# First FFN projection of a two-layer block: 20 pairs of column tiles by seven half-sized products, gated output in DRAM

## The chip, the cores and the metric

The kernel runs on one core of a Trainium2 chip, as one launch. The metric is device time in microseconds (us) of a whole execution. The core has a matrix engine (TensorE, "PE" in the profile, with its weight loads as "PEld"), three engines for element-wise work (VectorE "DVE", ScalarE "ACT", GpSimd "POOL") and SyncE ("SP"), whose queue ("SPq") issues all the DMAs of this kernel. TensorE writes its results to PSUM, from where DVE and ACT read them.

## The reference

Two blocks run one after the other on x of 1024 tokens by 1024 features, in float32. The first block is a gated mixer with convolutions, the second one has attention, a spatial gating unit and a feed-forward network (FFN). The change is in the FFN at the very end:

```python
def conv_gated_mlp(h, w_up, conv_w, conv_b, w_down):
    z = h @ w_up                                  # [1024, 1024] @ [1024, 5632]
    zp = jnp.pad(z, ((0, 0), (CONV_WIDTH - 1, 0), (0, 0)))
    zc = conv_b
    for tap in range(CONV_WIDTH):                 # 3 taps along the tokens
        zc = zc + conv_w[tap] * zp[:, tap:tap + S]
    gate, val = jnp.split(zc, 2, axis=-1)
    return (jax.nn.silu(gate) * val) @ w_down     # [1024, 2816] @ [2816, 1024]
...
x = x + conv_gated_mlp(rmsnorm(x, ffn_norm[l]), w_up[l], conv_w[l], conv_b[l], w_down[l])
```

## The kernel before

Features lie on the 128 partitions, tokens along the free dimension. Every float32 operand of TensorE is held as a pair hi + lo of a reduced type: hi is a rounded copy made by ACT, lo is the difference made by DVE (`hilo`, L110). A product of two such operands is three matmuls, hi hi, hi lo and lo hi (`mm3`), each 128x128 by 128x512.

The work is a list of slots (`Slot`), which `run` walks in order, and each engine executes its instructions in the order in which they are written; nothing is moved by a planner. A slot has weights to fetch (`ws`), matmuls (`mm`), an epilogue (`epi`) and a few hooks (`pre`, `mid`), and it can take some tasks from a queue of background work after its matmuls (`bg`). Weights run ahead of use: `dma_ahead` keeps two raw tiles in flight on SP, and `split_ahead`, called at the start of each slot, splits the weights of the slot after the next one into hi and lo, once their two buffers are free. Work that has been written earlier into DVE's or ACT's order stands ahead of such a split.

The FFN begins in the last part of the output phase of the second block. The first three column tiles of `w_up` (gate 0, value 0, gate 1) are done in halves of 512 tokens, slots uh0.0, uh1.0, uh2.0, uh0.1, uh1.1 and uh2.1, with the last transpose of H (the normalised input, as hi and lo, `self.H`) after uh0.0. Then tile up1.1 and 40 further tiles follow, gate and value in turn, 22 of each in all. Each is 2 halves x 8 k-blocks x 3 = 48 matmuls into one pair of PSUM banks (`pair`, 128x1024). Its epilogue `up_epi` is an ACT pass that applies one tap with the bias (z), two DVE passes for the other taps (L108), and then Silu on ACT for a gate or, for a value tile, the multiplication with its gate into `G` on DVE (L1435; the last one on POOL). `G` holds all 22 gated tiles of 128x1024 in on-chip memory (SBUF).

The down projection (`down`) takes two halves of 512 tokens with 22 steps each. A step splits one half row of `G` (gh, gl) and one row of `w_dn` (wh, wl), and adds 24 matmuls to eight PSUM banks, three pairs and two single banks (`bank`). At the end of a half the residual is added and the result stored.

Of the kernel before, what the change touches and what calls it, by code (L numbers as in the profile page):

```python
# [20 lines left out]
H = 512  # L21
# [30 lines left out]
class Slot:  # L52
    def __init__(self, ws=(), mm=None, epi=None, pre=None, bg=0, split=None, mid=None, dst=None,
                 name=""):
        self.dst = dst
        self.name = name
        self.mid = mid
        self.post = False
        self.ws = list(ws)
        self.mm = mm  # L60
        self.epi = epi
        self.pre = pre
        self.bg = bg
        self.split = split


class Kernel:
# [7 lines left out]
    def pool(self, name, bufs=1, **kw):  # L75
        return self.tc.tile_pool(name=name, bufs=bufs, **kw)

# [74 lines left out]
    def mm3(self, out, a, b, first, last):  # L152
        (ah, al), (bh, bl) = a, b
        self.mul(out, ah, bh, start=first, stop=False)
        self.mul(out, ah, bl, start=False, stop=False)
        self.mul(out, al, bh, start=False, stop=last)
# [17 lines left out]
    def bank(self):  # L174
        return self.pp.tile([P, H], F, tag="pm", name="pm", bufs=2)

    def run(self):
# [8 lines left out]
        def dma_ahead():  # L186
            while st["dma"] < len(reqs) and st["dma"] < st["split"] + N_RAW:
# [3 lines left out]
                self.nc.sync.dma_start(t[:, :n], reqs[r][1])  # L191
                raws[r] = t
                st["dma"] += 1

        def split_ahead(ahead=N_HL):
            while st["split"] < min(len(reqs), st["used"] + ahead):
# [20 lines left out]

        self.release = release
        self.dma_ahead, self.split_ahead, self.hl = dma_ahead, split_ahead, hl
        for i, s in enumerate(slots):  # L220
            if s.pre:
                s.pre()
            split_ahead()
# [17 lines left out]

    def setup(self):
        nc, I, ctx = self.nc, self.I, self.ctx
        self.pp = ctx.enter_context(self.pool("psum", 3, space=bass.MemoryType.PSUM))
        self.dram = ctx.enter_context(self.pool("dram", 1, space=bass.MemoryType.DRAM))
        self.cp = ctx.enter_context(self.pool("const"))
        self.ws = ctx.enter_context(self.pool("ws"))
# [22 lines left out]
    def body(self):  # L270
        self.setup()
        self.block1()
        self.block2()
        self.ffn()
        self.run()
        self.ca.close()
        self.cb.close()

# [471 lines left out]
    def out_phase(self, blk):  # L750
# [665 lines left out]

    def up_epi(self, f, side, ps):
        nc = self.nc
        if self.G is None:
            self.G = []  # L1420
            self.reopen("cf", "cgc")
            ga, gb = self.big("B1", F), self.big("A0", F)
            gc = self.base.tile([P, 6, 1024], F, name="gc")
            self.G = [g[:, i] for g, n in ((gc, 6), (ga, 8), (gb, 8)) for i in range(n)]
        ct = f + NF * side
        z = self.c1.tile([P, 1024], F, tag="z%d" % side, name="z", bufs=2)
        w = lambda k: self.par("conv_w", ct * 3 + k)
        self.act(z, ps, AF.Identity, bias=self.par("conv_b", ct), scale=w(2))
        self.stt(z[:, 1:1024], ps[:, 0:1023], w(1), z[:, 1:1024], ALU.mult, ALU.add)
        self.stt(z[:, 2:1024], ps[:, 0:1022], w(0), z[:, 2:1024], ALU.mult, ALU.add)  # L1430
        if side == 0:
            self.act(z, z, AF.Silu)
            self.zg = z
        else:
            (nc.vector if f < NF - 1 else nc.gpsimd).tensor_tensor(self.G[f], self.zg, z, ALU.mult)  # L1435

    def ffn(self):
        nc, I = self.nc, self.I
        self.G = None
        for n in range(3, 2 * NF):  # L1440
            f, side = n // 2, n % 2
            s = {}

            def mm(w, s=s):
                s["ps"] = self.pair()
                self.mm_std(s["ps"], w, *self.H)

            self.slots.append(Slot([I["w_up"][f + NF * side]], mm, mid=self.last_half if n == 3 else None,
                                   epi=lambda f=f, side=side, s=s: self.up_epi(f, side, s["ps"]), name="up%d.%d" % (f, side)))

        st = {}

        def down(hf, fs):
# [4 lines left out]
            def split(f):  # L1458
                gh = self.c1.tile([P, H], R, tag="gh", name="gh", bufs=2)
                gl = self.c1.tile([P, H], R, tag="gl", name="gl", bufs=2)  # L1460
                self.hilo(gh, gl, self.G[f][:, hs])
                g[f] = (gh, gl)
# [8 lines left out]
            def mm(*ws):  # L1471
                if fs[0] == 0:
                    prs = [self.pair() for _ in range(3)]
                    o = [pr[:, i * H:(i + 1) * H] for pr in prs for i in range(2)]
                    st["o"] = o[:4] + [self.bank(), self.bank()] + o[4:]
# [9 lines left out]

            def pre():
                if fs[0] == NF - 6:
# [4 lines left out]
            def epi():  # L1492
                if not end:
                    return
                for b in range(8):
                    if b == 5 and hf == 0:
# [7 lines left out]
                                   split=[lambda f=f: split(f) for f in fs], name="dn%d.%d" % (hf, fs[0])))  # L1504

        def open_d():
            self.reopen("cd")

# [88 lines left out]
```

## Time and profile before

| | us |
|---|---|
| time of three runs: median (lowest to highest) | 2809.13 (2806.71 to 2809.36) |
| profiled execution: span from its first to its last instruction | 2806.2 |
| TensorE busy in that span | 2765.9 (99%) |
| DVE busy | 1390.0 (50%) |
| ACT busy | 813.3 (29%) |
| half slots of the first FFN tiles and up1.1, 2084.0 to 2122.2 | 38.2 |
| the 40 column tiles from up2.0 on, 2122.2 to 2557.4 | 435.2 |
| down projection, from 2557.4 to its last matmul at 2801.4 | 244.0 |

The profile gives of the profiled execution its span; its own time, with what lies around the span, is not recorded apart from it. The median of the three runs is 2.9 us above the span.

In timeline rows the columns are start in us, duration in us, engine, line, operation, output tile <- input tiles, shapes and count; in brackets stands how long the engine had been idle and what released it. Consecutive instructions of a kind are merged into one row. Rows of groups give count, busy time and the mean of one in ns, then idle time ahead of them. Rows of stretches give for PE, PEld, DVE, ACT and POOL the busy us and the count, then the granted TensorE clock as a share of full speed, the share of DMA engines busy and GB/s. "pp" is a pair of PSUM banks, "pm" a single one. A and B are the large SBUF buffers, here the hi and lo part of H.

### The profile page before, as it was taken

Reading aid. Unit: us, or ns where it says so; the run is one execution under the profiler, and the core shown is the slowest. Engines: PE = TensorE matmul, PEld = TensorE weight load, DVE = VectorE, ACT = ScalarE, POOL = GpSimd, SP = SyncE. Lnnn points to the kernel's source line nnn. Section 1 sums busy time; section 2 is a strip of 40 time slices with the busy share of each in tenths; the row PEclk is TensorE's granted clock in tenths of the full one; section 3 lists DMA queues with packets and bytes.
Section 4 is the critical chain, followed back from the end, with each engine's and each line's share of the span. In section 5 each row is a group of like instructions: output and inputs, shape, how many; then the busy total and the mean of one; then the engine's idle time right before and its main releaser. Section 6 shows DMA issues by size and latency. Waiting matters only on the chain.

```text
span 2806.2 us, 29345 instructions
## 1 busy us (share of the span) xinstructions
PE 2765.9 (99%) x12420; PEld 2277.9 (81%) x12420; DVE 1390.0 (50%) x1450; ACT 813.3 (29%) x1038; POOL 139.9 (5%) x132
## 2 busy tenths in 40 slices
PE   5999999999999999999999999999999999999999
PEld 3888888888888888888887788888888888887887
DVE  6898888841244422532474255537634343433343
ACT  6322222221122211421343255532322222222222
POOL 4010000000000000000032100000000000000000
PEclk9999999999999999999999999999999999999999
DMA  5111111112111233221332222113521111112333
GB/s 226 46 68 53 61 53 53 60 70 73 64 49 49 94 118 115 105 83 68 109 139 77 76 75 76 48 48 132 188 82 57 46 45 53 46 53 68 128 127 129
DMA packets 66661, 232.08 MB, mean 83 GB/s; under 512 B 7521, under 2 KB 8033, under 8 KB 66530
## 3 DMA queue, kind: packets, MB, share of 16 engines
q1 hardware_dynamic: 66530, 230.20, 23.6%
q8 instruction: 98, 1.61, 0.2%
q14 instruction: 33, 0.27, 0.0%
HBM read 196.62 MB, written 33.55 MB: 82 GB/s over the span
## 4 chain that ended last, share of the span: by engine, by line
PE 94%; DVE 2%; issue 1%; ACT 1%; POOL 1%; DMA 0%; POOLq 0%; SPq 0%; DVEq 0%; ACTq 0%
PE pp L89 90%; PE pm L89 3%; PE pp L92 1%; PE pm L92 1%; ACT oj L102 0%; DVE A L105 0%; DVE wl L105 0%; POOL ox L867 0%; DVE ox L105 0%; DVE B L281 0%; DVE s L105 0%; DMA B<-in_xt 0%; DMA wr<-in_w_out 0%; ACT wh L111 0%; DVE w2l L105 0%
## 5 line engine op out<-in xcount | busy, mean ns | idle before, releaser
L89 PE MATMUL pp<-A,wh 128*128 128x512 f32 x4832 | 1552.8, 391 | 12.9 <-DVE A L105 8.3
L89 PE MATMUL pp<-A,wl 128*128 128x512 f32 x2768 | 1078.5, 390 | 0.3 <-DVE wl L105 0.2
L89 PEld LDWEIGHTS pp<-A,wh 128*128 128x128 f32 x4832 | 904.8, 188 | 207.9 <-DVE A L105 9.9
L105 DVE TENSOR_TENSOR wl<-wr,wh 128x1024 fp32r<-128x1024 f32 (+1 forms) x268 | 323.5, 1207 | 597.7 <-ACT wh L111 596.1
L89 PEld LDWEIGHTS pp<-A,wl 128*128 128x128 f32 x2768 | 520.1, 188 | 109.9 <-DVE wl L105 1.2
L89 PE MATMUL pp<-B,wh 128*128 128x512 f32 x1600 | 549.9, 389 | 0.0
L111 ACT CAST wh<-wr 128x1024 fp32r<-128x1024 f32 (+1 forms) x268 | 271.4, 1013 | 420.0 <-PE pp L89 415.1
L89 PEld LDWEIGHTS pp<-B,wh 128*128 128x128 f32 x1600 | 299.8, 188 | 62.0
L108 DVE SCALAR_TENSOR_TENSOR h<-p,par_t,h 128x1024 f32<-128x1024 f32 x240 | 309.4, 1289 | 7.7
L108 DVE SCALAR_TENSOR_TENSOR z<-pp,par_t,z 128x1023 f32<-128x1023 f32 x88 | 112.8, 1282 | 223.6 <-ACT z L102 222.0
L89 PE MATMUL pp<-B,wl 128*128 128x512 f32 x448 | 174.3, 389 | 0.0
L102 ACT ACTIVATE z<-pp,par_t 128x1024 f32<-128x1024 f32 x44 | 53.1, 1207 | 277.1 <-PE pp L89 277.1
L89 PE MATMUL pp<-B,A 128*128 128x512 f32 x480 | 132.3, 394 | 0.5 <-DVE B L105 0.3
L105 DVE TENSOR_TENSOR mg<-pp,mg 128x1024 f32<-128x1024 f32 x24 | 29.4, 1224 | 168.2 <-PE pp L89 168.2
L89 PEld LDWEIGHTS pp<-B,A 128*128 128x128 f32 x480 | 89.5, 188 | 20.6 <-DVE B L105 1.5
L89 PE MATMUL pp<-wh,gl 128*128 128x512 f32 x264 | 103.6, 392 | 2.0 <-DVE gl L105 1.9
L89 PE MATMUL pp<-wl,gh 128*128 128x512 f32 x264 | 103.4, 392 | 0.2 <-DVE wl L105 0.2
L89 PE MATMUL pp<-wh,gh 128*128 128x512 f32 x264 | 103.5, 392 | 0.0
L89 PEld LDWEIGHTS pp<-B,wl 128*128 128x128 f32 x448 | 84.1, 188 | 17.5
L102 ACT ACTIVATE mg<-pp,par_t 128x1024 f32<-128x1024 f32 x24 | 26.8, 1117 | 219.9 <-PE pp L89 219.8
L102 ACT ACT_TABLE_LOAD x55 | 70.6, 1283 | 52.8 <-PE pp L89 48.6
L102 ACT ACTIVATE B<-pp 128x1024 f32<-128x1024 f32 (+1 forms) x33 | 30.5, 923 | 149.7 <-PE pp L89 149.7
(248 smaller groups left out, 2022.2 us busy)
## 6 DMA issues: line engine op xcount, KB each, us to landing
wr<-in_w_in SPq DMA_DIRECT2D x129, 512.0 KB, 3.3
wr<-in_w_up SPq DMA_DIRECT2D x47, 512.0 KB, 3.3
wr<-in_w_dn SPq DMA_DIRECT2D x44, 512.0 KB, 3.3
wr<-in_w_br SPq DMA_DIRECT2D x24, 512.0 KB, 3.5
m_sp<-mg SPq DMA_DIRECT2D x16, 512.0 KB, 2.8
mi<-m_sp SPq DMA_DIRECT2D x16, 512.0 KB, 5.0
wr<-in_w_out SPq DMA_DIRECT2D x16, 512.0 KB, 3.3
x_sp<-ox SPq DMA_DIRECT2D x16, 512.0 KB, 2.9
```

Source lines behind the costliest of these rows:

```text
L89: self.nc.tensor.matmul(*a, **k)
L92: self.nc.tensor.transpose(*a)
L102: self.nc.scalar.activation(out, in_, func, **kw)
L105: self.nc.vector.tensor_tensor(out, a, b, op)
L108: self.nc.vector.scalar_tensor_tensor(out, a, s, b, op0, op1)
L111: self.nc.scalar.copy(hi, src)
```

## The change

The 20 pairs of column tiles f = 2 to 21 (gate f and value f together, 1024 rows by 256 columns of `w_up`, 1024 tokens) are computed as a 2x2 block product by a variant of Strassen's scheme: seven products of half size in every dimension, each 4 k-blocks x 3 matmuls, in place of eight. It has these parts:

- `open_ffn`, a new slot after the last transpose of H: it opens the memory of the FFN and puts 16 background tasks (`sums_of`, four tasks for each of four k-blocks) and the loads of the first two weight pairs into the background queue. The tasks make four combinations of the quarters of H and split them into hi and lo (`sh`). The five half slots after it take up to four of these tasks each (`bg = 4`).
- `two_first` makes, after up1.1, the operands a and b of the first pair. Operands a and d are parts of the raw weights, b and c are made of four sums of weight quarters (`two_sums`).
- PSUM is reopened as four pairs, without single banks (`open_psum`).
- `run_two` does one pair: products 1, 6, 5, 2, 7, 3, 4 into the four banks g1 to g4 of two pair tiles x and y. In between stand the copy e0 of g1 on ACT, five combinations on DVE (e1, e2, g4, g3, g2), the splits for this and the next pair, the loads for the pair after the next, and the epilogue tasks of the pair before (`old`).
- `up_tasks` holds the epilogue of `up_epi` as single tasks. Its last one multiplies on DVE and stores the gated tile to DRAM (`G_sp`) from SP's queue. `G` in SBUF is gone.
- In the last pair, `last_two` opens the weight buffers of the down projection and fetches and splits the first row there; the epilogue of this pair then runs at once. Weight loads of the down projection are held until then (`limit`), all but the first until `open_d`.
- `down` loads half rows of `G_sp` four steps ahead, and its eight banks are four pairs.

Tiles uh0 to uh2 and up1.1 are computed as before.

```diff
+    def open_psum(self, pairs, banks):
+        self.psum_stack.close()
+        self.psum_stack = ExitStack()
+        self.pp = self.psum_stack.enter_context(
+            self.pool("psum%d" % pairs, pairs, space=bass.MemoryType.PSUM, reuse_waits="tile"))
+        self.n_banks = banks
 
...
+    def sums_of(self, xh, xl, dst, scratch):
+
+        tasks = []
+        for k in range(4):
+            s = {}
+
+            def whole(k=k, s=s):
+                s["f"], s["s"] = scratch()
+                self.tt(s["f"], xh[:, k::4].bitcast(F), xl[:, k::4].bitcast(F), ALU.add)
+
+            def first(s=s):
+                f, t = s["f"], s["s"]
+                self.tt(t[:, 1], f[:, 0, H:], f[:, 1, H:], ALU.subtract)
+                self.tt(t[:, 3], f[:, 0, :H], f[:, 0, H:], ALU.subtract)
+
+            def second(s=s):
+                f, t = s["f"], s["s"]
+                self.tt(t[:, 2], t[:, 1], f[:, 0, :H], ALU.subtract)
+                self.tt(t[:, 0], t[:, 2], f[:, 1, :H], ALU.add)
+
+            def split(k=k, s=s):
+                self.hilo(dst[0][:, :, k], dst[1][:, :, k], s["s"])
+
+            tasks += [whole, first, second, split]
+        return tasks
+
+    def operands(self, xh, xl, sums):
+
+        quarter = lambda k, t: tuple(x[:, 4 * k:4 * k + 4, t * H:(t + 1) * H] for x in (xh, xl))
+        part = lambda n: tuple(x[:, n] for x in sums)
+        return {1: quarter(0, 0), 2: quarter(1, 0), 4: quarter(1, 1),
+                3: part(0), 5: part(1), 6: part(2), 7: part(3)}
+
+    def two_load(self, n):
+        if n < len(self.twos):
+            t = self.twos[n]
+            t.raw = self.wp.tile([P, 2048], F, tag="raw", name="raw", bufs=2)
+            for i, ap in enumerate(t.aps):
+                self.nc.sync.dma_start(t.raw[:, 1024 * i:1024 * (i + 1)], ap)
+
+    def two_sums(self, n, part):
+        if n >= len(self.twos):
+            return
+        t = self.twos[n]
+        q = t.raw.rearrange("p (n c) -> p n c", n=4)
+        if part == 0:
+            t.sums = self.wp.tile([P, 4, H], F, tag="sums", name="sums")
+            self.tt(t.sums[:, 1:3], q[:, 0::3], q[:, 2].unsqueeze(1).broadcast_to([P, 2, H]), ALU.add)
+        else:
+            self.tt(t.sums[:, 0], t.sums[:, 1], q[:, 3], ALU.add)
+            self.tt(t.sums[:, 3], t.sums[:, 0], q[:, 1], ALU.add)
+
...
+    def two_hi(self, n, which):
+        if n < len(self.twos):
+            t, src = self.two_part(n, which)
+            t.__dict__[which] = self.two_tile(which)
+            self.nc.scalar.copy(t.__dict__[which][0], src)
+
+    def two_lo(self, n, which):
+        if n < len(self.twos):
+            t, src = self.two_part(n, which)
+            hi, lo = t.__dict__[which]
+            self.tt(lo, src, hi.bitcast(F), ALU.subtract)
+
+    def two_begin(self):
+        self.two_load(0)
+        self.two_load(1)
+
+    def two_first(self):
+        self.two_hi(0, "a")
+        self.two_lo(0, "a")
+        self.two_sums(0, 0)
+        self.two_sums(0, 1)
+        self.two_hi(0, "b")
+        self.two_lo(0, "b")
+
+    def run_two(self, n):
+        t = self.twos[n]
+        x, y = self.pair(), self.pair()
+        g1, g2, g3, g4 = x[:, :H], x[:, H:], y[:, :H], y[:, H:]
+        later = deque(self.twos[n - 1].todo if n else ())
+        e = self.c1.tile([P, 3, H], F, tag="two", name="two")
+
+        def product(out, op, which, off, first):
+            (wh, wl), (xh, xl) = t.__dict__[which], self.X7[op]
+            for k in range(4):
+                ws = slice(off + k * P, off + (k + 1) * P)
+                self.mm3(out, (wh[:, ws], wl[:, ws]), (xh[:, k], xl[:, k]),
+                         first and k == 0, k == 3, skip_group_check=True)
+
+        def old(k):
+            for _ in range(min(k, len(later))):
+                later.popleft()()
+
+        product(g1, 1, "a", 0, True)
+        self.two_hi(n, "c")
+        old(2)
+        self.act(e[:, 0], g1)
+        product(g2, 6, "b", 0, True)
+        old(1)
+        self.two_lo(n, "c")
+        self.two_hi(n, "d")
+        self.tt(e[:, 1], g2, e[:, 0], ALU.add)
+        product(g3, 5, "b", H, True)
+        self.two_lo(n, "d")
+        self.two_hi(n + 1, "a")
+        self.two_sums(n + 1, 0)
+        self.tt(e[:, 2], g3, e[:, 0], ALU.subtract)
+        product(g1, 2, "a", H, False)
+        if n == len(self.twos) - 1:
+            self.last_two()
+        self.two_load(n + 2)
+        self.two_sums(n + 1, 1)
+        self.two_lo(n + 1, "a")
+        old(1)
+        product(g2, 7, "c", 0, False)
+        self.two_hi(n + 1, "b")
+        old(2)
+        self.tt(g4, e[:, 2], g2, ALU.subtract)
+        product(g3, 3, "d", 0, False)
+        self.two_lo(n + 1, "b")
+        old(1)
+        self.tt(g3, g3, e[:, 1], ALU.subtract)
+        product(g2, 4, "c", H, False)
+        old(len(later))
+        self.tt(g2, g2, e[:, 0], ALU.add)
+        t.todo = t.epi(x, y)
+        if n == len(self.twos) - 1:
+            for f in t.todo:
+                f()
+
...
+            add(Slot(pre=self.open_ffn))
+            for x in nxt[1:]:
+                x.bg = 4
...
+    def open_ffn(self):
+        self.reopen("cf", "")
+        self.wp = self.c1
+        self.sh = [self.big(n, R).rearrange("p k (h t) -> p (k h) t", h=2).rearrange(
+            "p (n k) t -> p n k t", n=4) for n in ("B1", "A0")]
+        self.G_sp = self.dram.tile([NF, P, 1024], F, name="g_sp")
+        wc = [self.wp.tile([P, 1024], R, name="wc%d" % j) for j in range(2)]
+        wa, wb = [[], []], []
+        wd = [self.A1[:, 8192 + i * H:8192 + (i + 1) * H] for i in range(2)]
+        count = [0]
+
+        def tile(which):
+            if which in "ab" and not wb:
+                p, = self.open_right("wab")
+                for i in range(2):
+                    wa[i] += [p.tile([P, 1024], R, name="wa%d%d" % (i, j)) for j in range(2)]
+                wb.extend(p.tile([P, 1024], R, name="wb%d" % j) for j in range(2))
+            if which == "a":
+                count[0] += 1
+                return wa[(count[0] + 1) % 2]
+            return {"b": wb, "c": wc, "d": wd}[which]
+
+        self.two_tile = tile
+        self.X7 = self.operands(*self.H, self.sh)
+
+        def scratch():
+            return (self.wp.tile([P, 2, 1024], F, tag="raw", name="f", bufs=2),
+                    self.wp.tile([P, 4, H], F, tag="sums", name="s"))
+
+        self.bgq.extend(self.sums_of(*self.H, self.sh, scratch))
+        self.bgq.append(self.two_begin)
+
+    def up_tasks(self, f, side, ps, st):
+        ct = f + NF * side
+        w = lambda k: self.par("conv_w", ct * 3 + k)
+
+        def first():
+            z = st[side] = self.c1.tile([P, 1024], F, tag="z%d" % side, name="z")
+            self.act(z, ps, AF.Identity, bias=self.par("conv_b", ct), scale=w(2))
+
+        def tap(k):
+            z = st[side]
+            self.stt(z[:, 2 - k:1024], ps[:, 0:1022 + k], w(k), z[:, 2 - k:1024], ALU.mult, ALU.add)
+
+        def last():
+            if side == 0:
+                self.act(st[0], st[0], AF.Silu)
+            else:
+                self.tt(st[1], st[0], st[1], ALU.mult)
+                self.nc.sync.dma_start(self.G_sp[f], st[1])
+
+        return [first, lambda: tap(1), lambda: tap(0), last]
+
...
     def ffn(self):
         nc, I = self.nc, self.I
-        self.G = None
-        for n in range(3, 2 * NF):
-            f, side = n // 2, n % 2
-            s = {}
-
-            def mm(w, s=s):
-                s["ps"] = self.pair()
-                self.mm_std(s["ps"], w, *self.H)
-
-            self.slots.append(Slot([I["w_up"][f + NF * side]], mm, mid=self.last_half if n == 3 else None,
-                                   epi=lambda f=f, side=side, s=s: self.up_epi(f, side, s["ps"]), name="up%d.%d" % (f, side)))
+
+        def mm3up(w):
+            self.ps3 = self.pair()
+            self.mm_std(self.ps3, w, *self.H)
+
+        self.slots.append(Slot([I["w_up"][1 + NF]], mm3up, mid=self.last_half, bg=-1,
+                               epi=lambda: self.up_epi(1, 1, self.ps3), name="up1.1"))
+        self.slots.append(Slot(pre=self.two_first))
+        self.slots.append(Slot(pre=lambda: self.open_psum(4, 0)))
+
+        def epi_of(f):
+            def epi(x, y):
+                st = {}
+                g, v = self.up_tasks(f, 0, x, st), self.up_tasks(f, 1, y, st)
+                return [g[0], g[1], g[2], lambda: (g[3](), v[0]()), v[1], v[2], v[3]]
+            return epi
+
+        for f in range(2, NF):
+            slot = Slot(name="up%d" % f)
+            slot.two = Two(I["w_up"][f], I["w_up"][f + NF], epi_of(f))
+            self.slots.append(slot)
 
         st = {}
+
+        def last_two():
+            _, self.first_g = self.open_right("ws", "g0")
+            t = st["g", 0, 0] = self.first_g.tile([P, H], F, name="gr0")
+            nc.sync.dma_start(t, self.G_sp[0][:, 0:H])
+            self.limit += 1
+            self.split_ahead()
+
+        self.last_two = last_two
 
...
+            def load(f, half):
+                t = st["g", half, f] = self.c1.tile([P, H], F, tag="gr", name="gr", bufs=6)
+                nc.sync.dma_start(t, self.G_sp[f][:, half * H:(half + 1) * H])
+
             def pre():
+                ahead = 4
+                for f in fs if (hf, fs[0]) != (0, 0) else ():
+                    if f + ahead < NF:
+                        load(f + ahead, hf)
+                    elif hf == 0:
+                        load(f + ahead - NF, 1)
...
         def open_d():
             self.reopen("cd")
+            self.limit = 1 << 30
+            for f in range(1, 5):
+                t = st["g", 0, f] = self.c1.tile([P, H], F, tag="gr", name="gr", bufs=6)
+                nc.sync.dma_start(t, self.G_sp[f][:, 0:H])
 
```

More of the change, by code (lines that the diff above doesn't have):

```diff
@@ L64, in __init__ @@
         self.split = split
+        self.two = None
+        self.hold = False
+class Two:
+    def __init__(self, a, b, epi):
+        self.aps, self.epi = (a, b), epi
 class Kernel:
@@ L174, in bank @@
     def bank(self):
-        return self.pp.tile([P, H], F, tag="pm", name="pm", bufs=2)
+        if not self.n_banks:
+            return self.pair()[:, 0:H]
+        return self.pp.tile([P, H], F, tag="pm", name="pm", bufs=self.n_banks)
     def run(self):
@@ L216, in release @@
             split_ahead()
+        held = next((i for i, s in enumerate(slots) if s.hold), None)
+        self.limit = first_req[held] if held is not None else len(reqs)
         self.release = release
         self.dma_ahead, self.split_ahead, self.hl = dma_ahead, split_ahead, hl
+        self.twos = [s.two for s in slots if s.two]
+        n_two = 0
         for i, s in enumerate(slots):
@@ L1472, in mm @@
                 if fs[0] == 0:
[L1473 to L1475 removed]
+                    prs = [self.pair() for _ in range(4)]
+                    st["o"] = [pr[:, i * H:(i + 1) * H] for pr in prs for i in range(2)]
                 if not end:
```

65 lines of the change are left out of this document (37 added, 28 removed).

## The prediction

> **What bounds the kernel now.** I read the page's head and its chain of waits first, then busy time by stretch, then the groups of the stretch that the change replaces.
>
> ```profile
> span 2806.2 us, 29345 instructions
> ...
> PE 94%; DVE 2%; issue 1%; ACT 1%; POOL 1%; DMA 0%; POOLq 0%; SPq 0%; DVEq 0%; ACTq 0%
> ...
> 2122.20:2557.40 435.20, 435.20 (x1922) 360.36 (x1920) 174.93 (x141) 107.50 (x101) 0.00 (x0) 1.00 0.15 49
> ```
>
> The stretch row (PE, weight loads, DVE, ACT, POOL busy; clock; DMA) is exactly the 40 column tiles that become 20 pairs. TensorE never rests in it, at full clock: 1920 matmuls in 435.2 us, 0.2267 us each. DVE is 40% busy. So any matmul taken out counts in full, as long as nothing else gets in TensorE's way.
>
> **The matmuls removed.** A tile pair is 2 x 48 matmuls now; seven products of 4 x 3 make 84. 20 x 12 x 0.2267 = **-54.4 us**; a pair then lasts 19.04 us and a product 2.72.
>
> **Does DVE keep up in a pair?** Steps from start to start:
>
> ```profile
> 2109.78 2.60 DVE L108 SCALAR_TENSOR_TENSOR z<-pp,par_t,z 128x1023 f32<-128x1023 f32 x2
> 2112.41 1.23 DVE L1435 TENSOR_TENSOR gc<-z 128x1024 f32<-128x1024 f32 x1
> 2113.55 1.22 DVE L105 TENSOR_TENSOR wl<-wr,wh 128x1024 fp32r<-128x1024 f32 x1
> ...
> 2564.84 0.69 DVE L105 TENSOR_TENSOR gl<-gc,gh 128x512 fp32r<-128x512 f32 x1 [2.27 <-POOL A L1435]
> 2565.45 1.22 DVE L105 TENSOR_TENSOR wl<-wr,wh 128x1024 fp32r<-128x1024 f32 x1
> ...
> L102 ACT ACTIVATE z<-pp,par_t 128x1024 f32<-128x1024 f32 x40 | 48.3, 1207 | 272.7 <-PE pp L89 272.7
> L111 ACT CAST wh<-wr 128x1024 fp32r<-128x1024 f32 x40 | 41.4, 1036 | 0.0
> L102 ACT ACTIVATE z<-z 128x1024 f32<-128x1024 f32 x20 | 21.2, 1061 | 54.6 <-DVE z L108 54.6
> ...
> L111 ACT CAST gh<-gc 128x512 fp32r<-128x512 f32 x1 | 0.6, 614 | 0.0
> ```
>
> A tap takes 1.31, a 1024-wide two-tensor operation 1.14, a 512-wide one 0.61. Per pair: 4 taps 5.2, the product of gate and value 1.1, low parts of a, b, c and d 4.0, weight sums 2.4, five combinations of products 3.1: 15.8 of 19.04 us. DVE would not bind by volume. Laid out in program order, the old pair's taps, the low parts and e1, e2 all fall inside the products that cover them; half by half the tightest point is g4, done some 1.3 us before product 4 needs it. ACT has 7.8 us: three copies, two halves (the copy of d, and g1), two z, one Silu. A free step thus costs 0; if DVE were 10% slower, that margin would be gone.
>
> **New waits inside a pair.** The seven sums live in two pair tiles, x (g1, g2) and y (g3, g4), and engines now read one half while TensorE goes on to the other half. Nothing in the kernel before does that, so the rows show only the neighbouring case, reading one half after both are written:
>
> ```profile
> 2674.10 0.39 PE L89 MATMUL pp<-wh,gl 128*128 128x512 f32 x1
> ...
> 2675.46 0.39 PE L89 MATMUL pp<-wh,gl 128*128 128x512 f32 x1
> ...
> 2675.88 1.29 DVE L105 TENSOR_TENSOR xo<-pp,xo 128x512 f32<-128x512 f32 x2 [2.53 <-PE pp L89]
> ...
> 2084.02 0.48 PE L89 MATMUL pp<-A,wh 128*128 128x512 f32 x1
> ...
> 2085.42 1.28 DVE L105 TENSOR_TENSOR B<-pm,A 128x512 fp32r<-128x512 f32 x2
> ```
>
> The first half of this pair got its last matmul at 2674.10, the second at 2675.46. DVE sat idle for 2.53 us and read the first half only at 2675.88, when the second was done. So the program orders accesses to a pair as a whole. (In the other memory it goes by region: the matmul at 2084.02 reads halves of H while other columns of H are still to be written at 2085.42.) Held to the same order, product 6 (g2) must wait until ACT has copied g1, and product 3 (g3) until DVE has written g4, which itself needs product 7.
>
> ```profile
> 2557.17 0.39 PE L89 MATMUL pp<-A,wl 128*128 128x512 f32 x1
> ...
> 2557.60 1.21 ACT L102 ACTIVATE z<-pp,par_t 128x1024 f32<-128x1024 f32 x1 [4.43 <-PE pp L89]
> ...
> 2558.84 2.60 DVE L108 SCALAR_TENSOR_TENSOR z<-pp,par_t,z 128x1023 f32<-128x1023 f32 x2 [4.33 <-ACT z L102]
> ...
> L102 ACT ACTIVATE B<-pp 128x512 f32<-128x512 f32 x8 | 4.8, 597 | 29.2 <-PE pp L89 29.2
> ...
> L105 DVE TENSOR_TENSOR xo<-pp,xo 128x512 f32<-128x512 f32 x12 | 7.7, 686 | 8.1 <-PE pp L89 8.1
> ```
>
> A reader starts 0.43 us after the last matmul's start, 0.20 after its slot. Product 6 waits 0.20 + 0.60 + 0.06 = 0.86 us; product 3 waits 0.20 + 0.69 + 0.06 = 0.95 (0.06: the low part at 2564.84 + 0.69, its matmul at 2565.59 below). Behind them queues all later TensorE work. 20 x 1.81 = **+36.2 us**. Bounds: 0, if halves are kept apart, and 50, if writing g4 back into PSUM, which no row shows, takes DVE twice its 0.69. I take 36.2, by the row at 2675.88.
>
> **The start of the stretch.** New DVE work stands ahead of the weight splits in DVE's own queue: four rounds of sums of H, one per half slot. A round: one 2048-wide addition 2.2 (1.14 + 2 x 0.53), four 512-wide 2.4, then DVE waits for ACT's 2048-wide copy 1.9 (1.04 + 2 x 0.42), then the low part 2.2, and only then the next slot's weight low part 1.1: 9.9 us for a slot of 24 matmuls, 5.44. From 2086.7 (the row at 2085.42 ends) four rounds and the first tile's two taps end at 2086.7 + 39.5 + 2.6 = 2128.8; then tile up1.1's weights are ready, and it runs 10.9 us. The clock matters too:
>
> ```profile
> 2563.26 0.39 PE L89 MATMUL pp<-wl,gh 128*128 128x512 f32 x1
> ...
> 2565.59 0.66 PE L89 MATMUL pp<-wh,gl 128*128 128x512 f32 x1 [1.94 <-DVE gl L105]
> ...
> 2565.80:2569.20 3.40, 3.40 (x9) 2.65 (x9) 1.47 (x2) 0.00 (x0) 0.00 (x0) 0.50 0.46 133
> ...
> 46.69 0.66 PE L92 MATMUL pm<-cst,B 128*128 128x128 f32 x4 [1.22 <-ACT u L102]
> ...
> 48.63 0.62 PE L89 MATMUL pp<-A,wh 128*128 128x512 f32 x2
> ...
> 49.09 0.39 PE L89 MATMUL pp<-A,wl 128*128 128x512 f32 x1
> ```
>
> After 1.94 us without work the granted clock was 0.50 for 3.4 us, a loss of half of that, 1.7; after 1.22 us matmuls kept 0.23 us spacing. up1.1 begins after a wait of some 7 us: +1.7. It ends near 2141.4; then act 1.4, two taps 2.6, the multiply 1.1, low part of a 1.1: product 1 starts near 2147.7 instead of 2122.2. Product 6 then needs the weight sums, the copy and low part of b, 4.6 us, or product 1 at half clock, 5.4, against 2.7. Sum 25.5 + 2.7, and a little for hand-overs between dependent operations: **+29 us**. Bounds: 11 (DVE's 49.4 us of steps from 2086.7 without any wait, against 2124.9) and 35 (a halved window in each of the starved slots). Product 1 of the first pair itself needs only the raw loads, which follow the store of the first gated row on SP; they land before 2141 and are hidden.
>
> **The end of the stretch.** The last pair's epilogue now runs at once, and the loads of gated rows 1 to 4 and of the second down weight stand behind its store on SP. SP keeps order:
>
> ```profile
> SPq L855 <- DVE ox L105: 64.3, 8, 11.9
> ...
> 2067.45 0.32 SPq L855 DMA_DIRECT2D x_sp<-ox  x1
> 2067.89 0.35 SPq L782 DMA_DIRECT2D ox<-x_sp  x1
> ...
> L191 SPq DMA_DIRECT2D wr<-in_w_dn x44: 327/328/340, 2532.2 to 2782.4; - x44
> ...
> wr<-in_w_dn SPq DMA_DIRECT2D x44, 512.0 KB, 3.3
> ...
> 8.00:16.00 8.00, 4.05 (x7) 1.04 (x6) 6.41 (x12) 7.25 (x14) 3.92 (x9) 1.00 1.02 414
> ```
>
> Counted from the last product: g2 0.9, act 1.2, taps 2.6, Silu 1.1, act 1.2, taps 2.6, multiply 1.2 = 10.9, then store and four loads issued (5 x 0.33), then the weights, 3.3 to landing: 15.9. Copy 1.1, low part 1.2, gl 0.7 (needed 0.5 after the first matmul): the second down slot starts at 18.4 instead of 5.4. That is 13.0, with one halved window 14.7. Before, this place lost 3.8 us already, which goes:
>
> ```profile
> 2563.24 1.05 ACT L111 CAST wh<-wr 128x1024 fp32r<-128x1024 f32 x1 [2.98 <-PE pp L89]
> ...
> 2572.52 1.05 ACT L111 CAST wh<-wr 128x1024 fp32r<-128x1024 f32 x1 [7.72 <-PE pp L89]
> ```
>
> The rows are one slot apart, 9.28 instead of 5.44. Net **+11 us**. Bounds: 2 (only the last pair's PSUM tiles hold up the first down slot, until 10) and 16 (2.5 MB at the 414 GB/s of the stretch 8 to 16, and a second halved window). The first down weight and gated row are loaded during the last pair; their splits delay g4 there, +1.5. In the rest of the down projection 768 KB per 5.44 us is 145 GB/s, a third of 414: 0. The gated stores, 512 KB a pair, are hidden likewise.
>
> **Sum.** -54.4 + 36.2 + 29 + 11 + 1.5 = +23.3; 2806.2 + 23.3 = 2829.5 as a span. The three runs' median is 2.9 above the profiled span: **2832.4 us**.
>
> **Rivals.**
> A, the forecast: pair order, 62%. Its own range 2818 to 2850, from the bounds of the start, the end and g4.
> B, halves independent, the side of faster: product 6 and product 3 start at once, the 36.2 falls away, 2796.2 (2786 to 2807 by the same bounds). It is decided at one place, the first matmul of product 6: below 0.2 us of wait it is B. For it: the region order of H; against it: the read at 2675.88. 26%. The Trainium skill, "PSUM — Partial Sum Buffer", section on PSUM bank collisions, asks for ordering by bank and quadrant and found accesses to different banks of one quadrant to run clean together; each half is one bank, so by that rule B's 2796 would be allowed. The row at 2675.88 does not agree that this program makes use of it.
> C, also the starting work is hidden, because ACT and DVE get at it earlier than I lay out: 2796.2 less 29 = 2767. Against it: H is complete only at 2086.7. 5%.
> D, the short waits halve the clock again and again: one halved window per pair, 20 x 1.7 on A, 2866. Against it: after 1.22 us nothing happened, and A's waits are below 1. 7%. The Trainium skill, "TensorE: Matmul & The Clock Gate", section "A second HAM failure mode: psum-queue depth-cycling", says that micro-idles between matmul groups cost throughput by re-throttling, which is D; its table of advice puts the drop at gaps over about 3 us, while here 1.94 was enough, so the measurement stands.
>
> **How the numbers follow.** No change is +-0.2%, 2803.5 to 2814.7, what a measurement here can tell apart. Faster: C and nearly all of B but its upper end, 0.27. Same: that upper end and A's lowest, 0.06. Slower: the rest of A, and D, 0.67. The range 2790 to 2852 leaves out C, D, the lowest part of B and a little of A: about 0.2.
>
> **What would show it.** In the pair stretch: TensorE idle before product 6 with ACT as releaser and before product 3 with DVE, 0.9 us each, and pairs 20.85 us apart (B: 19.04, none). Matmuls down by 240. At the start: uh0.1 to up1.1 each waiting for a weight low part, 2 to 8 us, granted clock 0.5 in places. At the end: SP idle until the last multiply, then a burst, and a wait of some 8 us before the second down slot. If DVE's busy share in the stretch came out near 100%, the volume count is wrong; if the starting waits are under 15 us in all, the order of the sums is.

## The result and the profile after

The changed kernel takes 2852.05 us (median of 4 runs, 2848.3 to 2853.09) against 2809.24 before (4 runs): a ratio of 1.0155, interval 1.014 to 1.0169. It is slower, as forecast, but by 42.8 us where 23.3 were forecast. The profiled execution has a span of 2851.3 us, 45.1 above the one before. The page's head, the stretches (columns as for before: PE, PEld, DVE, ACT, POOL, then clock), and the waits of TensorE between 2084 and 2620, where the columns are the total in us, the number of waits and the longest:

```profile
span 2851.3 us, 29350 instructions
...
PE 2741.4 (96%) x12180; PEld 2239.4 (79%) x12180; DVE 1565.5 (55%) x1675; ACT 862.7 (30%) x1102; POOL 137.0 (5%) x131
...
PE 87%; DVE 7%; issue 2%; ACT 2%; DMA 1%; POOL 1%; SPq 0%; DVEq 0%; ACTq 0%; POOLq 0%
```

```profile
2084.70:2155.90 71.20, 52.81 (x183) 39.16 (x181) 53.93 (x47) 24.20 (x23) 0.00 (x0) 0.81 0.19 67
...
2179.20:2562.70 383.50, 352.94 (x1512) 280.99 (x1512) 287.58 (x306) 134.04 (x145) 0.00 (x0) 1.00 0.20 74
...
2582.00:2620.00 38.00, 22.90 (x80) 16.92 (x79) 13.14 (x13) 7.96 (x9) 0.00 (x0) 0.76 0.32 111
```

```profile
PE pp L110 <- DVE pp L126: 23.2, 20, 4.1
PE pp L110 <- ACT two L123: 13.8, 20, 0.7
PE pp L110 <- ACT gh L132: 9.7, 1, 9.7
PE pp L110 <- DVE z L129: 9.4, 3, 4.0
PE pp L110 <- DVE wl L126: 6.4, 4, 1.8
PE pp L110 <- ACT wh L132: 6.2, 3, 3.3
PE pp L110 <- DVE wa L126: 1.1, 1, 1.1
```

The first two rows are the pairs: 20 waits for DVE's write of g4, 20 for ACT's copy of g1, in every pair. One of the waits for g4, that of the last pair, took 4.1 us. The other rows are the start (wl, wh, wa and 4.0 us of z) and the end (gh and the other 5.3 us of z). The second stretch holds 18 regular pairs of 21.31 us. Seven products need 19.04, so 40.8 us are lost there; as idle time it shows 383.5 - 352.9 = 30.6. Where the other 10.2 lie can be read around two of the waits:

```profile
2190.00 0.39 PE L110 MATMUL pp<-B,wc 128*128 128x512 f32 x1
2190.57 0.68 DVE L126 TENSOR_TENSOR pp<-two,pp 128x512 f32<-128x512 f32 x1
...
2191.40 0.47 PE L110 MATMUL pp<-B,A 128*128 128x512 f32 x1 [1.01 <-DVE pp L126]
2191.71 0.39 PE L110 MATMUL pp<-A,A 128*128 128x512 f32 x1
...
2199.46 0.39 PE L110 MATMUL pp<-A,wa 128*128 128x512 f32 x1
2200.53 0.50 PE L110 MATMUL pp<-B,wb 128*128 128x512 f32 x1 [0.69 <-ACT two L123]
2200.87 0.40 PE L110 MATMUL pp<-A,wb 128*128 128x512 f32 x1
```

Matmuls in a run start 0.227 us apart, but each row lasts 0.39, and the idle time is counted from its end. Product 3 starts 1.40 after the matmul ahead of it, 1.17 more than a slot; product 6 starts 1.07 after, 0.85 more than a slot. And the second matmul behind each wait starts 0.31 and 0.34 after the first, 0.1 late again. Start and end, the long waits of TensorE in order of time, and at the end what ACT and SP did:

```profile
2128.63 0.50 PE L110 MATMUL pp<-A,wh 128*128 128x512 f32 x1 [3.35 <-ACT wh L132]
2131.14 0.79 PE L110 MATMUL pp<-A,wl 128*128 128x512 f32 x1 [1.78 <-DVE wl L126]
2148.32 0.76 PE L110 MATMUL pp<-A,wa 128*128 128x512 f32 x1 [4.02 <-DVE z L129]
2150.62 1.22 PE L110 MATMUL pp<-A,wa 128*128 128x512 f32 x2 [1.11 <-DVE wa L126]
2155.94 0.79 PE L110 MATMUL pp<-B,wb 128*128 128x512 f32 x1 [0.69 <-ACT two L123]
...
2578.03 0.77 PE L110 MATMUL pp<-B,A 128*128 128x512 f32 x1 [4.09 <-DVE pp L126]
2591.13 0.47 PE L110 MATMUL pp<-wh,gh 128*128 128x512 f32 x1 [2.10 <-DVE z L129]
2596.01 0.47 PE L110 MATMUL pp<-wh,gh 128*128 128x512 f32 x1 [3.25 <-DVE z L129]
2607.67 0.79 PE L110 MATMUL pp<-wh,gh 128*128 128x512 f32 x1 [9.75 <-ACT gh L132]
```

```profile
wr<-in_w_dn SPq DMA_DIRECT2D x1, 512.0 KB, 5.0
...
2556.69 0.72 SPq L214 DMA_DIRECT2D wr<-in_w_dn  x1
...
2570.60 0.39 PE L110 MATMUL pp<-B,wa 128*128 128x512 f32 x1
...
2571.03 1.05 ACT L132 CAST wh<-wr 128x1024 fp32r<-128x1024 f32 x1 [7.81 <-PE pp L110]
...
2572.50 1.06 ACT L123 ACTIVATE z<-z 128x1024 f32<-128x1024 f32 x1
...
2574.68 2.60 DVE L129 SCALAR_TENSOR_TENSOR z<-pp,par_t,z 128x1023 f32<-128x1023 f32 x2 [0.74 <-ACT z L123]
2577.20 0.68 DVE L126 TENSOR_TENSOR pp<-two,pp 128x512 f32<-128x512 f32 x1
...
2606.05 1.04 ACT L132 CAST wh<-wr 128x1024 fp32r<-128x1024 f32 x1 [12.82 <-DMA wr<-in_w_dn]
...
2597.15 0.32 SPq L1643 DMA_DIRECT2D g_sp<-z  x1
2597.57 2.32 SPq L1757 DMA_DIRECT2D gr<-g_sp  x4
2599.94 8.77 SPq L214 DMA_DIRECT2D wr<-in_w_dn  x3
```

The first row gives the time of that one load from issue to landing. In the last pair ACT stood idle for 7.81 us ahead of its copy of the first down weight. It did not wait for the load, which was issued at 2556.69 and had landed 5.0 us later, at 2561.7. The row names TensorE: the copy starts 0.43 us after the matmul at 2570.60, the last one of product 2 that reads the high part of weight operand a, since `last_two` opens the buffers of the down weights in the place of these operands. Behind the copy, in ACT's order, stood the Silu of the pair before and the next z, behind z the taps on DVE, and behind the taps g4, at 2577.20; product 3 waited 4.09 us for it. At the end the store of the last gated row goes out at 2597.15, the four row loads and the second weight behind it, and that weight is there only at 2606.05: 9.75 us of TensorE.

### The profile page after: what moved, and what is told of

Read it like the earlier page. It is cut to its first block, busy times and chain, and to the rows that moved or that the text cites. A ratio compares the mean times of both kernels' runs of the same rounds, so it can differ in the third digit from the quotient of the medians.

```text
span 2851.3 us, 29350 instructions
## 1 busy us (share of the span) xinstructions
PE 2741.4 (96%) x12180; PEld 2239.4 (79%) x12180; DVE 1565.5 (55%) x1675; ACT 862.7 (30%) x1102; POOL 137.0 (5%) x131
## 4 chain that ended last, share of the span: by engine, by line
PE 87%; DVE 7%; issue 2%; ACT 2%; DMA 1%; POOL 1%; SPq 0%; DVEq 0%; ACTq 0%; POOLq 0%
PE pp L110 85%; DVE z L129 2%; DVE wa L126 1%; PE pm L110 1%; PE pp L113 1%; PE pm L113 1%; DVE s L126 1%; DVE wl L126 1%; ACT oj L123 0%; DVE pp L126 0%; DVE A L126 0%; DVE two L126 0%; ACT two L123 0%; DVE sums L126 0%; ACT B L132 0%
## 5 line engine op out<-in xcount | busy, mean ns | idle before, releaser
L110 PE MATMUL pp<-A,wh 128*128 128x512 f32 x4192 | 1307.1, 392 | 19.1 <-DVE A L126 8.3
L110 PEld LDWEIGHTS pp<-A,wh 128*128 128x128 f32 x4192 | 786.3, 188 | 191.1 <-DVE A L126 9.9
L110 PE MATMUL pp<-A,wl 128*128 128x512 f32 x2128 | 832.5, 391 | 6.7 <-DVE wl L126 6.6
L110 PEld LDWEIGHTS pp<-A,wl 128*128 128x128 f32 x2128 | 401.6, 189 | 93.4 <-DVE wl L126 9.6
L110 PE MATMUL pp<-B,wh 128*128 128x512 f32 x960 | 303.6, 392 | 0.7 <-DVE sy L129 0.7
L110 PEld LDWEIGHTS pp<-B,wh 128*128 128x128 f32 x960 | 181.3, 189 | 38.5 <-issue 0.9
L110 PE MATMUL pp<-B,A 128*128 128x512 f32 x640 | 188.5, 399 | 23.6 <-DVE pp L126 23.2
L110 PE MATMUL pp<-B,wb 128*128 128x512 f32 x320 | 105.7, 402 | 13.8 <-ACT two L123 13.8
L110 PE MATMUL pp<-A,wa 128*128 128x512 f32 x320 | 107.1, 396 | 5.1 <-DVE z L129 4.0
L110 PEld LDWEIGHTS pp<-wh,gh 128*128 128x128 f32 x352 | 66.7, 190 | 30.5 <-ACT gh L132 10.5
```

The lines of the kernel that those rows point to most:

```text
L110: self.nc.tensor.matmul(*a, **k)
```

## The experiments

**Four single PSUM tiles (e1), and only the value side apart (e2).**

```diff
-        x, y = self.pair(), self.pair()
-        g1, g2, g3, g4 = x[:, :H], x[:, H:], y[:, :H], y[:, H:]
+        x, y = (self.half(), self.half()), (self.half(), self.half())
+        g1, g2, g3, g4 = *x, *y
...
+                for h, p in enumerate(ps):
+                    a, b = h * H + 2 - k, min(1024, (h + 1) * H + 2 - k)
+                    self.stt(z[:, a:b], p[:, 0:b - a], w(k), z[:, a:b], ALU.mult, ALU.add)
```

`half` gives a PSUM tile of one bank; the down projection takes eight of them in place of its four pairs. In e2 the first two lines keep `x = self.pair()`.

> The changed kernel with the four sums of a pair in four PSUM tiles of one bank each, and the epilogue's reads of PSUM done half by half (four more taps on DVE and two more activations on ACT per pair); nothing else differs. Theory 'order by PSUM tile': products 6 and 3 wait only because the tile of two banks is ordered as a whole, so both waits go, and with them the slow second matmul behind each; the period of a pair falls from 21.31 us to 19.04 to 19.3, 20 pairs save 40 to 45 us, and the whole takes about 2809 us (2804 to 2814). Rival 'late readers': ACT and DVE are late anyway, so the waits only move (to product 4, which needs g4, or to the next pair's product 1), DVE has yet more to do, the period stays above 20.5 and the time above 2835.

> Only the value side (g3 and g4) in two PSUM tiles of one bank each; the gate side (g1 and g2) stays one tile of two banks. By 'order by PSUM tile' product 3's wait goes and product 6's stays. It tells the price of one such wait: if it is the idle time in the trace alone, 20 x 1.0 = 20 us are saved, 2831; if the second matmul behind each wait also costs its 0.33 us, 20 x 1.34 = 27, 2824. By 'late readers' TensorE waits for g4 ahead of product 4 instead, and the time stays at 2850.

e1 took 2799.67 us (8 runs), a ratio to before of 0.9969, interval 0.9958 to 0.998; that is 52.4 less than the change as it stood. e2 took 2822.81, ratio 1.0049 (1.0034 to 1.0064). A stretch of 18 pairs of e1, and the wait for g1 that e2 keeps:

```profile
2173.80:2516.50 342.70, 342.70 (x1513) 283.76 (x1513) 291.89 (x379) 142.29 (x180) 0.00 (x0) 1.00 0.22 82
```

```profile
PE pp L110 <- ACT two L123: 13.8, 20, 0.7
```

In e1 TensorE does not rest once in 18 pairs of exactly 19.04 us, though DVE, busy for 85% of it, has more to do than in the change. So the waits came from the order by whole PSUM tiles, and 'late readers' falls. In e2 the row of g4 is gone and that of g1 stays; its regular pairs last 20.02 us. So the wait ahead of product 3 cost 21.31 - 20.02 = 1.29 us with 1.01 of idle time, and the one ahead of product 6 cost 0.98 with 0.69; the first is close to the 1.34 of e2's expectation. Each costs some 0.28 more than its idle time, the 0.16 by which a row outlasts its slot and the 0.1 of the late second matmul. In the spans, 2851.3 and 2798.0, e1 won 8 us more than the 45.4 of these waits (20 x 2.27). In the last pair g4 is late in e1 too, but there it holds up only product 4, by 1.78 us of idle time, and from product 6 to the first down matmul it takes 18.44 us instead of 23.39; and the first pair takes 19.68 instead of 23.28. Beyond the 1.29 and 2.27 us of waits already counted in them, these two make 5 of the 8 us.

**Without the sums of H (e3).**

```diff
-        self.bgq.extend(self.sums_of(*self.H, self.sh, scratch))
+        self.bgq.extend([lambda: None] * 16)
...
-                3: part(0), 5: part(1), 6: part(2), 7: part(3)}
+                3: quarter(0, 0), 5: quarter(0, 1), 6: quarter(1, 0), 7: quarter(1, 1)}
```

> The sums of quarters of H are not formed; products 3, 5, 6 and 7 read quarters of H in their place, so the output is not the reference's, but all matmuls, weight sums, waits in the pairs and the epilogue stay. Theory 'DVE queue at the start': the time from the first matmul of uh1.0 to product 6 of the first pair falls from 71.2 us to about 48 (what stays beyond the 40.9 of the matmuls are the two taps and the low part of the first weights ahead of product 1, 5 us, and a window at half clock), and the whole to about 2828 (2824 to 2832). Rival: it is the changeover of PSUM or the loads that hold up the start, then the stretch stays above 62 and the time above 2842.

It took 2829.22 us, ratio 1.0074 (1.0059 to 1.0089). From the first matmul of uh1.0 to product 6 of the first pair:

```profile
2083.16:2133.15 49.99, 43.91 (x184) 34.91 (x182) 25.87 (x23) 16.91 (x19) 0.00 (x0) 0.93 0.26 95
```

That is 50.0 us instead of 71.2, with DVE busy for 25.9 instead of 53.9. The sums, with ACT's copies for them, make up 21.2 us of the 30.3 by which the start exceeds its 40.9 us of matmuls; the rest is two taps and a low part ahead of product 1 (4.0 and 1.4 us of waits), product 6's own wait, and the clock.

**Loads ahead of the last epilogue (e4).**

```diff
-            t = st["g", 0, 0] = self.first_g.tile([P, H], F, name="gr0")
-            nc.sync.dma_start(t, self.G_sp[0][:, 0:H])
-            self.limit += 1
+            for f in range(3):
+                t = st["g", 0, f] = self.first_g.tile([P, H], F, name="gr%d" % f)
+                if f == 1:
+                    self.limit += 2
+                    self.dma_ahead()
+                    self.limit -= 1
+                nc.sync.dma_start(t, self.G_sp[f][:, 0:H])
             self.split_ahead()
...
-            for f in range(1, 5):
+            for f in range(3, 5):
```

> The second down weight and gated rows 1 and 2 are loaded ahead of the last pair's epilogue, where row 0 is, instead of behind the last store; nothing else differs. Theory 'SP order at the end': the second down slot no longer waits for the load, only for DVE, which splits its weight and row behind the last multiply; it starts about 12.5 us after the last product's end instead of 21.5, a window at half clock goes too, and the time is about 2841 (2838 to 2844). Rival 'PSUM holds it': the first down slot's own waits for the last pair's tiles decide, and not more than 3 us are saved, 2848 or more.

It took 2842.33 us, ratio 1.0119 (1.0104 to 1.0134), 9.7 less than the change. The waits of TensorE at its end:

```profile
2588.80 0.47 PE L110 MATMUL pp<-wh,gh 128*128 128x512 f32 x1 [2.10 <-DVE z L129]
2593.68 0.47 PE L110 MATMUL pp<-wh,gh 128*128 128x512 f32 x1 [3.25 <-DVE z L129]
2604.36 0.49 PE L110 MATMUL pp<-wh,gh 128*128 128x512 f32 x1 [1.74 <-ACT gh L132]
```

The wait of 9.75 us is gone: the second slot starts 11.7 us after the last product, at 2595.47, instead of 21.5. Only 1.74 of it comes back at the third slot, whose weight still stands behind the store. The waits for PSUM, 2.10 and 3.25, are what the first slot had anyway. So it was SP's order, not PSUM. In the profiled execution 7.6 us of the gain lie between the first and the last down matmul (252.1 instead of 259.7).

**The first down split behind g4 (e8).** In `last_two`, `split_ahead` becomes `dma_ahead`, and the split is issued behind g4:

```diff
         self.tt(g4, e[:, 2], g2, ALU.subtract)
+        if n == len(self.twos) - 1:
+            self.split_ahead()
```

> The changed kernel with one thing moved: in the last pair the split of the first down weight and of gated row 0 is issued behind g4 instead of ahead of the older epilogue's Silu; their loads stay where they are. Theory 'ACT order in the last pair': Silu and the second z no longer stand behind a copy that waits for the load, so g4 is in time, product 3 waits 1.0 us instead of 4.1 and runs at full clock; from product 6 of the last pair to the first down matmul 17.6 us instead of 23.4, and the time is about 2846.5 (2844 to 2849). Rival: the split is then late itself, the first down slot waits for it, and less than 2 us are won, 2850 or more.

It took 2844.31 us, ratio 1.013 (1.0113 to 1.0147). The wait of product 3 in the last pair is now one of twenty equal ones, and from product 6 there to the first down matmul it takes 17.62 us instead of 23.39:

```profile
PE pp L110 <- DVE pp L126: 20.0, 20, 1.0
```

```profile
2566.89 1.05 ACT L132 CAST wh<-wr 128x1024 fp32r<-128x1024 f32 x1 [4.75 <-PE pp L110]
```

The copy itself starts no later: 8.26 us after product 6 here, 8.27 in the change, behind product 2 in both. So the theory's order on ACT is right, but the copy waits for its place in memory and not for the load. The time fell by 7.7 us, a little more than the 5.8 of the last pair; in the profiled execution the first pair also kept full clock this time (21.23 us instead of 23.28).

**A start and an end laid out otherwise (e5, e6), and both (e7).** All three have the single PSUM tiles of e1. e5 in short:

```diff
-            for x in nxt[1:]:
-                x.bg = 4
+            for x, n in zip(nxt[1:], (4, 2, 4, 1, 0)):
+                x.bg = n
...
+        flat = list(tasks[0][:4])
+        for k in range(1, 4):
+            flat += [tasks[k][0], tasks[k - 1][4], *tasks[k][1:4]]
...
+        self.bgq.extend(self.two_first())
...
+        for n in range(4, 6):
+            f, side = n // 2, n % 2
...
+                self.mm_std(st["ps"], w, *self.H)
...
-        for f in range(2, NF):
+        for f in range(3, NF):
```

The slots up2.0 and up2.1 are computed in the old way by this. e6 in short, in the last pair of `run_two`, where `last_split` splits one down weight and row:

```diff
+        if last:
+            self.last_two()
+            old(3)
         self.tt(e[:, 2], g3, e[:, 0], ALU.subtract)
...
         product(g2, 7, "c", 0, False)
+        if last:
+            act(0, 0)
+            self.last_split(self.nc.vector)
...
         self.tt(g4, e[:, 2], g2, ALU.subtract)
+        if last:
+            act(1, 1)
+            taps(0, 0)
...
         product(g2, 4, "c", H, False)
+        if last:
+            self.last_split(self.nc.gpsimd)
```

> The version with four single PSUM tiles a pair, and a start laid out otherwise: column tiles of f = 2 are computed in the old way (19 pairs are left), the four rounds of sums of H are spread over uh1.0 to up2.0 with the low part of a round one task behind ACT's copy, the first pair's weight loads and splits stand ahead of up2.1's epilogue, and the first pair takes PSUM tiles that no epilogue is still reading. Theory 'DVE queue at the start': no slot waits any more; from the first matmul of uh1.0 to product 6 of the first pair (f = 3) it takes 62.7 us of matmuls (40.9 and one old pair of 21.8) and at most 2 of waits, against 89.8 to product 6 of f = 3 in the version with four single tiles; the time falls from 2799.7 to about 2774 (2770 to 2780). Rival 'too much for DVE': DVE has some 27 us of sums more to do in 62 us, in which it was busy for 35 already, so the slots still wait, half of the loss stays, and the time is 2786 or more.

> The version with four single PSUM tiles a pair, and an end laid out otherwise: in the last pair the older epilogue goes first, its own epilogue starts with the sums that are complete (g1, g4, g3, then g2), the first two down weights and three gated rows are loaded from product 5 on and split by ACT, DVE and POOL during the last products, and the first down slot takes the PSUM tiles in the order in which they come free. Theory 'order on the queues': the first down slot and the second start without a wait; from product 6 of the last pair to the first down matmul 16.4 us (18.4), from there to the last matmul 240.5 us (258.8); the time falls from 2799.7 to about 2780 (2776 to 2785). Rival 'held by the data': the second down slot cannot start before the last gated row is stored and the epilogue is through on DVE, not more than 8 us are won, 2791 or more.

> All three together: four single PSUM tiles a pair, the spread start with 19 pairs, and the end laid out otherwise. If the three losses are separate, their gains add up: 2851.3 - 53 (tiles) - 26 (start) - 20 (end) gives a span of about 2753, the time 2754 (2748 to 2762), 2% below the kernel before. If they hide one another (the work that is moved away from one place is missed at the next), it stays above 2770.

e5 took 2778.74 us, ratio 0.9897 (0.9883 to 0.991); e6 2781.3, ratio 0.9906 (0.9893 to 0.992); e7 2758.39, ratio 0.9824 (0.9811 to 0.9838). From e1 that is 20.9, 18.4 and 41.3: the gains add up (to 39.3 by the first two), so the losses did not hide one another. Stretches and waits of e7:

```profile
2084.20:2150.60 66.40, 64.34 (x280) 51.25 (x278) 56.06 (x50) 26.73 (x25) 0.00 (x0) 1.00 0.24 87
2170.60:2494.20 323.60, 323.60 (x1429) 268.07 (x1428) 275.02 (x357) 134.28 (x170) 0.00 (x0) 1.00 0.22 81
2494.20:2552.00 57.80, 56.30 (x246) 45.80 (x246) 30.97 (x41) 20.47 (x27) 5.49 (x3) 1.00 0.47 159
```

```profile
PE pp L111 <- DVE wl L137: 1.3, 3, 0.5
PE ph L111 <- ACT gh L135: 1.2, 1, 1.2
PE pp L111 <- ACT wh L135: 0.6, 1, 0.6
PE ph L111 <- DVE wb L127: 0.5, 1, 0.5
PE ph L111 <- DVE wl L137: 0.2, 1, 0.2
```

The start has 2.1 us of idle time in 66.4, with one more old pair in it, and DVE does the same sums; the end has 1.5 in 57.8, with POOL taking three low parts. From 2084 to 2552 TensorE waits 3.8 us in all, against 70 in the change, and the clock is 1.00 in all three stretches. e5 came out 4.7 us above the middle of what was expected: its start took 66.4 us where at most 64.7 were, and from product 6 of its last pair to the first down matmul it took 20.48 us where e1 had 18.44, as the late g4 cost it 2.46 us of idle time ahead of product 4, and a window at half clock.

## Why the prediction was wrong in size, and right in kind

The 45.1 us of the two profiled spans, by the prediction's own terms:

| term | predicted | measured | from |
|---|---|---|---|
| matmuls removed | -54.4 | -54.4 | 240 fewer |
| waits in the pairs | +36.2 | +45.4 | 20 x (1.29 + 0.98) |
| start, first pair included | +29 | +31.3 | 71.2 - 40.9 - 0.98, and 2.0 of half clock in the first pair |
| last pair | +1.5 | +5.8 | 23.4 - 16.3 (six products) - 1.29 |
| end | +11 | +15.6 | first to last down matmul 259.7, before 244.0 |
| elsewhere | 0 | +1.4 | |
| sum | +23.3 | +45.1 | |

*Matmuls, DVE's volume.* Right: 12180 of 12420 matmuls, and DVE was no bound.

*Waits in the pairs.* The mechanism was right, and e1 and e2 show it: case A, not B (nor C, for which the start would have to be hidden too). The reading of the row at 2675.88, that a pair of banks is ordered as a whole, held for writes as well. The term "20 x 1.81" was mis-sized. Product 6's wait is 0.85 beyond the slot, as forecast (0.86); product 3's is 1.17 and not 0.95, since DVE was still at a tap of the older pair and took up g4 0.57 us after the last matmul's start instead of 0.43, and TensorE started 0.15 after its end instead of 0.06. And the late second matmul, 0.1 for each of 40 waits, wasn't in the sum at all. The Trainium skill, "PSUM — Partial Sum Buffer", section on PSUM bank collisions, allows different banks to run together; e1 agrees, at 19.04 us a pair without a wait. That rule told what the change could have had, the row what this program did.

*Start.* Right in cause, and to 2.3 us in size. The four rounds of sums on DVE ahead of the weight splits are the cause for 21.2 us (e3), and spreading them ends it (e5). That it came so close is in part luck. This execution reached uh1.0 0.7 us later than the one before; with that taken off, up1.1 ended 2.0 us later than worked out (at 2144.1), and product 1 began 4.2 us after it and not 6.3, since its first two matmuls do not need the low part of a. The 2.0 us not foreseen are one more window at half clock, at 2155.94 (the matmul of 0.79 us in the row above); in e3 and e8 the first pair did not have it.

*Last pair.* The step "their splits delay g4 there, +1.5" failed. It counted the splits' own time, and no wait ahead of them. But ACT works in the order of the program: its copy stood idle for 7.81 us, until product 2 had read the buffer whose place the down weight takes, the Silu and the next z stood behind it, g4 came 3.1 us late, and product 3 then ran at a clock of 0.50. The step came to 5.8 us. e8 moved this one split behind g4, and 17.62 us came out instead of 23.39.

*End.* The mechanism, SP's order, is shown by e4 and e6. The second down slot started 21.5 us after the last product, not 18.4. The multiply was over at 10.98 (10.9 forecast); the four row loads took SP 0.58 us each and not 0.33, and the weight landed 6.1 us after its issue and not 3.3. The step had taken both from a calm stretch, and left the burst of 2.5 MB to the upper bound. Behind the wait the clock then stood at 0.50 for 6.5 us of matmuls (2607.67 to 2614.20), a loss of 3.3 us where one window of 1.7 was counted; that too was left to the bound.

*Rival D*, short waits that halve the clock again and again, did not come true: 36 waits in 18 pairs at a mean clock of 1.00. The Trainium skill, "TensorE: Matmul & The Clock Gate", section "A second HAM failure mode: psum-queue depth-cycling", has such micro-idles bring the throttle back; these, of 0.7 to 1.0 us every 9 to 12 us, did not. From 2084 us to the last matmul the clock falls to 0.50 in this trace only during a wait of more than 1.7 us or within 1.2 us behind one; behind waits of 1.53 (2097.87) and 2.10 us (2591.13) it stayed at 1.00.

The sum was 21.8 us short in the profiled spans, 19.6 in the medians. By terms: waits 9.2, end 4.6, last pair 4.3, start 2.3, elsewhere 1.4 (0.7 ahead of uh1.0, 0.7 behind the last down matmul). In the last pair a wait had been left out; the others are mis-sized, the waits in the pairs most. The estimates were taken from rows of calmer stretches, and each of these terms came out higher. The upper bounds of the pairs, the start and the end lie 13.8, 6 and 5 us above their estimates, which would together allow 2857; the range ended at 2852, just short of 2852.05. What stays open is why the second matmul behind a wait starts late; no run takes that apart.

## What to carry to other kernels

A scheme with fewer multiplications pays only as far as its new dependencies leave the matrix engine alone: here 54 us of matmuls were saved and 99 lost again in the pairs, at the start and at the end (the last pair with it), and in none of these places for the volume of extra additions. Give every partial sum its own tile of the unit in which the program orders accesses, spread preparatory work over slots with room for it, and issue loads and splits for the next stage ahead of the last epilogue, but put a split whose buffer is not free yet behind the work that is due; tiles, start and end were each worth about 20 to 50 us, and together they turned 1.0155 into 0.9824. Where several small waits are priced, count from slot to slot and add what stands behind the wait, and price an end of a stage with the queue's burst in it.

## What was not expected of the hardware

- A short wait of TensorE costs 0.28 us more than the idle time that the profile gives it: 1.29 for 1.01, 0.98 for 0.69. 0.1 of it is the second matmul, which starts 0.31 to 0.34 us after the first and not 0.23.
- One order of waits led to half clock of different length. Ahead of product 1 of the first pair TensorE waited 4.02 us in the change and in e8, and in both product 6 began 7.62 us behind product 1, after 0.69 us of idle time. In the change the clock stood at 0.50 from 2146.6 to 2160.2, so product 6 ran at half clock; in e8 it stood there from 2146.83 to 2153.66, and product 6 ran at 1.00. No run takes apart what decides it.
- With a burst of 2.5 MB on one queue (a store, four row loads and two weight loads issued within 3.7 us), a 512 KB load took 6.1 us to land, 3.4 in the median of all 44.
